# Pairing the projections of three rounds in one hybrid decoder layer: product 1 of two pairs in seven quarter products instead of eight

## The chip, the cores and the metric

One kernel launch on one core of a Trainium2 chip. The metric is the device time of one execution in microseconds; the times are medians of several executions. Engines are named as in the profile: PE is TensorE, DVE VectorE, ACT ScalarE, POOL GpSimd, SP the queue that issues most DMAs.

## The reference

One decoder layer on a prompt of 1024 tokens and 8 sample tokens (1032 columns in the kernel, activations transposed: model dimension on partitions), model width 1024, all in f32:

```python
x = layer_norm(ALPHA * x + 0.5 * swiglu(x, ffn1_wi, ffn1_wo), ...)
z = x @ w_in + b_in          # [q | k | v | o-gate | i | f | B | C | h | gate_a | gate_b], 1024 columns each but i, f (4)
y_a = (HeadLN(mLSTM(q, k / 16, v, i, f)) * sigmoid(o)) @ w_a
y_b = (B * conv3(C * h)) @ w_b                 # causal depthwise convolution over tokens, width 3
x = layer_norm(ALPHA * x + (sigmoid(g_a) * y_a + sigmoid(g_b) * y_b) @ w_mix, ...)
x = layer_norm(ALPHA * x + 0.5 * swiglu(x, ffn2_wi, ffn2_wo), ...)
x = layer_norm(ALPHA * x + sigmoid(x @ w_pg) * (p @ w_pp), ...)
```

The change lies in `z = x @ w_in + b_in`.

## The kernel before, in words

**Numbers.** A matmul of f32 operands is done on a high and a low part of each: `w = wh + wl`, `x = xh + xl`, and the three matmuls `wh*xh`, `wh*xl`, `wl*xh` into one accumulator (`product`, lines 575 to 577). A weight tile is split by a cast on ACT (high part) and a subtraction on DVE (low part), the "put" of that tile.

**Pairs.** A projection is done 256 output columns at a time. Such a *pair* is two blocks of 128 outputs, and `pair` (line 581) computes it by a 2x2 split in seven products instead of eight: `wcomb` makes seven weight combinations, the activations `XP` hold seven combinations of token columns, and each of the products 0 to 6 runs for two column blocks s = 0, 1 (256 and 260 columns). A product of one block is 4 row groups of 128 by 3 matmuls, so a pair has 7 x 2 x 12 = 168 matmuls.

**Pairs of pairs.** In the two feed-forward stages, for seven of the blocks each, `pair2` (line 627) does two pairs together (`wcomb2` makes their weights). Product 1 of both uses the same activations, so these two 12-matmul products in two column blocks (48 matmuls) are one 2x2 problem, which is split once more: seven *quarter* products of 6 matmuls, 42 in all, with four tiles of activation combinations `XQ`, which `quarters` builds beforehand on POOL, DVE and ACT. `pair2` accumulates a pair's parts in PSUM tiles `mm`, `aux` and `pn`, copies them to `sreg` or to the target by ACT, and adds later parts on DVE (line 637).

**The ring.** Weight tiles live in a ring of nine slots (`w0` to `w5`, `e0`, `e1`, `cd`), handed out in program order (`slot`). A slot can be filled again when its last reader is done. `XQ` takes three of them (`QS`: `w4`, `w5`, `e0`), so the feed-forward stages run `pair2` on a ring of six.

**The rounds.** The projections q, k, v, B, C and h have four pairs each. Pair 0 of q and k is done first, then `conv(0)` (C, h, B of pair 0; C * h goes into `pre_`, the convolution `conv_y` on DVE makes `y` of it, B multiplies `y`) and `val(0)`. Then three rounds, h = 1, 2, 3, of six `pair` calls each:

```python
    for h in range(1, 4):
        conv(h)
        if h < 3:
            decays(4 * h - 4)
        lin(qscr, Q0, h, AF.Identity, sm=0)
        if h < 3:
            decays(4 * h - 2)
        lin(kscr, K0, h, AF.Identity, 1.0 / 16.0, 1)
        if h == 3:
            dec_pre()
            beside.extend([[] for _ in range(8)] + [[dec_dot]])
        val(h)
```

After them come twelve pairs for the output gate and the merge gates.

**What else uses the ring.** `ahead_all` puts 26 small jobs beside the steps of the rounds (list `beside`, one entry is taken after each product step): each loads a weight block of a later stage into a ring slot (line 192), splits it there (lines 184 and 185) and stores it in DRAM `wscr` (line 197). `decays` takes one slot, loads two broadcast rows (`gscr`), works on them on DVE (line 1359) and ACT, and stores them (`escr`). Since slots are handed out in program order, all jobs of one pair's steps stand in the ring between the weights of that pair and those of the next.

**What sets the order.** A scheduler that simulates the program orders each engine's instructions at build time; on the chip each engine then runs its list in order and waits where an operand is not ready.

Of the kernel before, what the change touches and what calls it, by code (L numbers as in the profile page):

```python
# [11 lines left out]
AF = mybir.ActivationFunctionType  # L12
# [51 lines left out]
def layer_kernel(ctx: ExitStack, tc: tile.TileContext, I, O):  # L64
# [30 lines left out]
    def tmp(n=BM):  # L95
        return tmpp.tile([128, BM], F32, name="tmp", tag="tmp")[:, :n]
# [48 lines left out]
    def use_ring(slots):  # L145
        set_ring([i for i in from_ring() if i in slots])
# [245 lines left out]
    def wcomb(raws):  # L392

        lo_, up = raws
        g = lo_.shape[1]
        a11, a21, a12, a22 = lo_[:, :, 0:128], lo_[:, :, 128:256], up[:, :, 0:128], up[:, :, 128:256]

        def put(src):
            s = slot()
            hi, lo = (s[:, i * 512:i * 512 + g * 128].rearrange("p (k n) -> p k n", n=128) for i in range(2))  # L400
            S.copy(hi, src)  # L401
            V.tensor_tensor(lo, src, F_(hi), op=OP.subtract)  # L402
            return hi, lo

        def fresh():
            return rawp.tile([128, 512], F32, name="raw", tag="raw")[:, :g * 128].rearrange("p (k n) -> p k n", n=128)

        s1, s2, s3 = fresh(), fresh(), fresh()
        out = [put(a11)]
        V.tensor_tensor(s1, a21, a22, op=OP.add)  # L410
        G.tensor_tensor(s3, a11, a21, op=OP.subtract)
        out.append(put(a12))
        V.tensor_tensor(s2, s1, a11, op=OP.subtract)
        out.append(put(s2))
        out.append(put(a22))
        out.append(put(s1))
        s4 = fresh()
        G.tensor_tensor(s4, a12, s2, op=OP.subtract)  # L418
        out.append(put(s3))
        out.append(put(s4))  # L420
        return out
# [66 lines left out]
    def bcol(c0, m):  # L488
        return col(c0 // 128 + m) if c0 < 4096 else col(32 + (c0 - CB0) // 128 + m)
# [516 lines left out]
    XP = x7()  # L1006
# [14 lines left out]
    def sg_pair():  # L1021
        if count["step"] == 0:
            return fixed
        i = 2 * (count["sg"] % 2)
        count["sg"] += 1
        return [gen(psgs[i + q]) for q in range(2)]

    def in_pair(c0):
        i = count["w"]
        count["w"] += 1  # L1030
        return wcomb(wraw(w_in, c0, [praws[1 + (2 * i + q) % 3] for q in range(2)] if count["step"] == 0 else
                          praws[i % 2 * 2:i % 2 * 2 + 2]))


    nT = sb.tile([128, 2, 32], F32, name="nT")
# [180 lines left out]
    def conv_y(j, pre, y):  # L1216
        S.activation(y, pre, AF.Identity, scale=cw(2, j), bias=cbias(j))
        yv, pv = v2(y), v2(pre)
        for sh in (1, 2):
            for d, src in ((yv[:, :, sh:512], pv[:, :, 0:512 - sh]), (yv[:, 1, 0:sh], pv[:, 0, 512 - sh:512])):  # L1220
                V.scalar_tensor_tensor(d, src, cw(2 - sh, j), d, op0=OP.mult, op1=OP.add)
        for r in (1, 0):
            V.scalar_tensor_tensor(smp(y), p24(cbuf[:, j, r:16:2]), cw(r, j), smp(y), op0=OP.mult, op1=OP.add)
        pl = stp.tile([128, 16], F32, name="st", tag="st")[:, 0:10]
        V.tensor_copy(pl[:, 0:2], pre[:, NT - 6:NT - 4])
        V.tensor_copy(p24(pl[:, 2:10]), smp(pre))
        pt = aux()
# [57 lines left out]
        xsums(XP[0], rp, 0, kp)  # L1285
    late_sums(XP[1], rp, ((12, 13, 14, 15), (16, 17, 18, 19)))

    def conv(jj, w=None):
        pre_ = sg_pair()

        def out_c(i, c, fn):
            fn(bs(pre_[i], c, BLK4))

        pair(w or in_pair(CC0 + jj * 256), XP, (0, 1), out_c, w is not None)
        for i in range(2):
            S.activation(pre_[i], pre_[i], AF.Identity, bias=bcol(CC0, 2 * jj + i))

        def out_h(i, c, fn):
            d, t = bs(pre_[i], c, BLK4), tmp(BN[c % 2])
            fn(t)  # L1300
            V.scalar_tensor_tensor(d, t, bcol(CH0, 2 * jj + i), d, op0=OP.add, op1=OP.mult)

        pair(in_pair(CH0 + jj * 256), XP, (0, 1), out_h)
        y = sg_pair()
        for i in range(2):
            conv_y(2 * jj + i, pre_[i], y[i])

        def out_b(i, c, fn):
            d, t = bs(y[i], c, BLK4), tmp(BN[c % 2])
            fn(t)  # L1310
            V.scalar_tensor_tensor(d, t, bcol(CB0, 2 * jj + i), d, op0=OP.add, op1=OP.mult)

        pair(in_pair(CB0 + jj * 256), XP, (0, 1), out_b)
        for i in range(2):
            DQ.dma_start(yscr[2 * jj + i], y[i])

    def lin(dst, c0, n, fn_, scale=1.0, sm=None):

# [11 lines left out]
        return d  # L1330

    def val(h):
        d = lin(None, V0, h, AF.Identity)
        for c in range(8):
            pt = aux(256)
            for i in range(2):
                T.transpose(pt[:, i * 128:(i + 1) * 128], d[i][:, ccol(c):ccol(c) + 128], ident)
            hi, lo = (tmpp.tile([128, BM], R, name="tmp", tag="tmp")[:, :256] for _ in range(2))
            hilo((hi, lo), pt)
            DQ.dma_start(vhscr[h, c], F_(hi))  # L1340
            DQ.dma_start(vlscr[h, c], F_(lo))
# [141 lines left out]

    beside.extend([partial(next, steps, None)] for _ in range(22))
    w_pg, w_pp = I["w_pg"][0], I["w_pp"][0]
    conv(0, w0)
    val(0)
    parts_ = [(w, k, n) for n in range(2) for w, kk in ((w_pg, 8), (w_pp, 2)) for k in range(kk)]
    parts_ += [(I["ffn2_wo"][0], k, n) for n in range(2) for k in (1, 20, 21)]
    ahead_all([w[k * 128:(k + 1) * 128, n * 512:(n + 1) * 512] for w, k, n in parts_], 14 * 14)  # L1490
    for h in range(1, 4):
        conv(h)
        if h < 3:
            decays(4 * h - 4)
        lin(qscr, Q0, h, AF.Identity, sm=0)
        if h < 3:
            decays(4 * h - 2)
        lin(kscr, K0, h, AF.Identity, 1.0 / 16.0, 1)
        if h == 3:
            dec_pre()  # L1500
            beside.extend([[] for _ in range(8)] + [[dec_dot]])
        val(h)

    if count["sg"] % 2:
        psgs = psgs[2:] + psgs[:2]
# [595 lines left out]
```

## Time and profile before

| | |
|---|---|
| median of 3 runs | 2658.96 us (2652.04, 2658.96, 2659.68) |
| profiled execution | 2652.47 us, of which the traced span is 2650.7 us, TensorE clock 0.999 |
| PE busy | 2617.7 us of the span (99%), 21684 matmuls |
| DVE, ACT, POOL busy | 1937.2 (73%), 1286.1 (49%), 686.0 (26%) us |
| three rounds of projections | about 846 to 1200 us after the span's start |
| feed-forward stage with `pair2` | about 140 to 415 us, and again about 1975 to 2250 us |

Busy time is the time in which an engine has an instruction in flight; where PE is busy all the time, the time of a stage is the number of its matmuls times their distance.

### The profile page before, as it was taken

Reading aid. Unit: us, or ns where it says so; the run is one execution under the profiler, and the core shown is the slowest. Engines: PE = TensorE matmul, PEld = TensorE weight load, DVE = VectorE, ACT = ScalarE, POOL = GpSimd, SP = SyncE. Lnnn points to the kernel's source line nnn. Section 1 sums busy time; section 2 is a strip of 40 time slices with the busy share of each in tenths; the row PEclk is TensorE's granted clock in tenths of the full one; section 3 lists DMA queues with packets and bytes.
Section 4 is the critical chain, followed back from the end, with each engine's and each line's share of the span. In section 5 each row is a group of like instructions: output and inputs, shape, how many; then the busy total and the mean of one; then the engine's idle time right before and its main releaser. Section 6 shows DMA issues by size and latency. Waiting matters only on the chain.

```text
span 2650.7 us, 56267 instructions
## 1 busy us (share of the span) xinstructions
PE 2617.7 (99%) x21684; PEld 2579.6 (97%) x21684; DVE 1937.2 (73%) x4239; ACT 1286.1 (49%) x2862; POOL 686.0 (26%) x694
## 2 busy tenths in 40 slices
PE   9999999999999999999999999999999999999998
PEld 9999999999999999999999999999999999999998
DVE  6867667987887758655555678658877667888787
ACT  5444446433554555546566555425544444533241
POOL 2432221112421111111110345323343223111354
PEclk9999999999999999999999999999999999999999
DMA  6333335532234556436667676821433233644421
GB/s 210 96 101 98 99 117 195 181 121 70 73 125 136 189 168 203 152 92 191 199 191 239 225 235 222 255 91 33 145 107 105 92 105 119 221 134 136 174 74 57
DMA packets 319990, 382.96 MB, mean 144 GB/s; under 512 B 29432, under 2 KB 247752, under 8 KB 319720
## 3 DMA queue, kind: packets, MB, share of 16 engines
q1 hardware_dynamic: 297400, 358.10, 41.9%
q10 hardware_dynamic: 22320, 21.26, 2.8%
q8 instruction: 170, 2.79, 0.4%
q14 instruction: 100, 0.82, 0.1%
HBM read 260.26 MB, written 119.05 MB: 143 GB/s over the span
## 4 chain that ended last, share of the span: by engine, by line
PE 85%; DVE 8%; DMA 3%; issue 2%; ACT 2%; POOL 1%; SPq 0%; DVEq 0%; ACTq 0%; POOLq 0%
PE mm L575 15%; PE mm L577 14%; PE mm L576 14%; PE aux L575 6%; PE aux L576 6%; PE aux L577 6%; PE mm L216 5%; PE mm L217 5%; PE mm L218 5%; PE pn L216 1%; PE pn L218 1%; PE pn L217 1%; DVE a L260 1%; DVE a L185 1%; DVE w L402 1%
## 5 line engine op out<-in xcount | busy, mean ns | idle before, releaser
L575 PE MATMUL mm<-a,w 128*128 128x260 f32 (+1 forms) x2348 | 664.2, 283 | 3.3 <-DVE a L878 2.3
L576 PE MATMUL mm<-a,w 128*128 128x260 f32 (+1 forms) x2348 | 660.8, 282 | 0.6 <-DVE a L260 0.5
L577 PE MATMUL mm<-a,w 128*128 128x260 f32 (+1 forms) x2348 | 659.5, 281 | 0.0
L575 PEld LDWEIGHTS mm<-a,w 128*128 128x128 f32 x2348 | 441.7, 188 | 12.2 <-issue 8.0
L576 PEld LDWEIGHTS mm<-a,w 128*128 128x128 f32 x2348 | 442.0, 188 | 1.1 <-DVE a L260 1.0
L577 PEld LDWEIGHTS mm<-a,w 128*128 128x128 f32 x2348 | 441.7, 188 | 0.8 <-issue 0.8
L418 POOL TENSOR_TENSOR raw<-a,raw 128x512 f32<-128x512 f32 (+2 forms) x70 | 86.5, 1236 | 857.8 <-issue 410.7
L575 PE MATMUL aux<-a,w 128*128 128x260 f32 (+1 forms) x814 | 230.7, 283 | 1.0 <-ACT a L259 0.8
L216 PE MATMUL mm<-a,w 128*128 128x260 f32 (+4 forms) x802 | 228.0, 286 | 2.7 <-ACT w L1594 1.9
L576 PE MATMUL aux<-a,w 128*128 128x260 f32 (+1 forms) x814 | 229.2, 282 | 0.0
L577 PE MATMUL aux<-a,w 128*128 128x260 f32 (+1 forms) x814 | 229.1, 281 | 0.0
L217 PE MATMUL mm<-a,w 128*128 128x260 f32 (+4 forms) x802 | 227.7, 285 | 0.6 <-POOL a L1637 0.6
L218 PE MATMUL mm<-a,w 128*128 128x256 f32 (+2 forms) x751 | 213.3, 285 | 0.2 <-DVE w L156 0.2
L575 PE MATMUL mm<-a,e 128*128 128x256 f32 (+1 forms) x681 | 192.8, 283 | 2.8 <-DVE a L878 1.7
L576 PE MATMUL mm<-a,e 128*128 128x256 f32 (+1 forms) x681 | 191.8, 282 | 0.0
L577 PE MATMUL mm<-a,e 128*128 128x256 f32 (+1 forms) x681 | 191.6, 281 | 0.0
L402 DVE TENSOR_TENSOR w<-raw,w 128x512 fp32r<-128x512 f32 (+2 forms) x190 | 129.7, 685 | 55.6 <-ACT w L401 55.3
L401 ACT CAST w<-raw 128x512 fp32r<-128x512 f32 (+2 forms) x190 | 108.8, 574 | 116.7 <-PE mm L577 43.3
L575 PEld LDWEIGHTS aux<-a,w 128*128 128x128 f32 x814 | 153.2, 188 | 3.7 <-issue 2.1
L216 PEld LDWEIGHTS mm<-a,w 128*128 128x128 f32 x802 | 150.8, 188 | 4.8 <-ACT w L1594 3.2
L577 PEld LDWEIGHTS aux<-a,w 128*128 128x128 f32 x814 | 153.3, 188 | 0.0
L576 PEld LDWEIGHTS aux<-a,w 128*128 128x128 f32 x814 | 153.3, 188 | 0.0
(607 smaller groups left out, 8070.8 us busy)
## 6 DMA issues: line engine op xcount, KB each, us to landing
a<-in_ffn_wi_dram SPq DMA_DIRECT2D x80, 512.0 KB
a<-in_w_in_dram SPq DMA_DIRECT2D x68, 512.0 KB
a<-hsum SPq DMA_DIRECT2D x119, 258.0 KB
hsum<-a SPq DMA_DIRECT2D x68, 258.0 KB
a<-in_ffn_wo_dram SPq DMA_DIRECT2D x40, 384.0 KB
wscr<-w SPq DMA_DIRECT2D x23, 512.0 KB
a<-in_state_C_dram ACTq DMA_DIRECT2D x32, 256.0 KB
out_dram<-a ACTq DMA_DIRECT2D x32, 256.0 KB
```

Source lines behind the costliest of these rows:

```text
L185: V.tensor_tensor(lo, F_(lo), F_(hi), op=OP.subtract)
L216: T.matmul(ps, wh, xh, start=(i == 0), stop=False)
L217: T.matmul(ps, wh, xl, start=False, stop=False)
L218: last = T.matmul(ps, wl, xh, start=False, stop=(i == n - 1))
L260: order_["lo"] = V.tensor_tensor(dst[1], src, F_(dst[0]), op=OP.subtract).ins
L401: S.copy(hi, src)
L402: V.tensor_tensor(lo, src, F_(hi), op=OP.subtract)
L418: G.tensor_tensor(s4, a12, s2, op=OP.subtract)
L575: T.matmul(ps, wh, xh, start=start and kp == 0, stop=False, skip_group_check=True)
L576: T.matmul(ps, wh, xl, start=False, stop=False, skip_group_check=True)
L577: T.matmul(ps, wl, xh, start=False, stop=stop and kp == len(xs) - 1, skip_group_check=True)
```

## The change

In the three rounds the six `pair` calls become three `pair2` calls: q with k (`keys`), C with h (inside `conv`), B with v (`conv_val`). `conv(0)` and `val(0)` stay as they were. `XQ` is built beside the B pair of `conv(0)` and `val(0)`, from where on the ring has six slots. Biases move into the copies out of PSUM, k's scale stays an ACT instruction per block, and `times` multiplies in place. After the rounds the ring gets its three slots back, and the part of `XP` that `quarters` overwrote is loaded again (from `x2scr`) and split, as `redo` does in the feed-forward stages.

```diff
+    def times(d, c0, n):
+        def end(i, c, t):
+            e = bs(d[i], c, BLK4)
+            V.scalar_tensor_tensor(e, t, bcol(c0, 2 * n + i), e, op0=OP.add, op1=OP.mult)
+        return end
...
-    def conv(jj, w=None):
+    def conv(jj, w=None, then=None):
         pre_ = sg_pair()
+        if w is None:
+            pair2(wcomb2(in_raw(CC0 + jj * 256), in_raw(CH0 + jj * 256)), XP, XQ, (whole(pre_), own),
+                  (done, times(pre_, CH0, jj)), (lambda i: bcol(CC0, 2 * jj + i), None))
+        else:
...
+    def conv_val(jj, y):
+        d = sg_pair()
+        pair2(wcomb2(in_raw(CB0 + jj * 256), in_raw(V0 + jj * 256)), XP, XQ, (own, whole(d)),
+              (times(y, CB0, jj), done), (None, lambda i: bcol(V0, 2 * jj + i)))
+        for i in range(2):
+            DQ.dma_start(yscr[2 * jj + i], y[i])
+        val_end(jj, d)
+
+    def keys(n):
+        q, k = sg_pair(), sg_pair()
...
+        pair2(wcomb2(in_raw(Q0 + n * 256), in_raw(K0 + n * 256)), XP, XQ, (whole(q), whole(k)), (done, scaled),
+              (lambda i: bcol(Q0, 2 * n + i), None))
+        lin_store(qscr, q, n, 0)
+        lin_store(kscr, k, n, 1)
...
+    late = quarters(XP)
+    XQ = []
+    def then():
+        use_ring([i for i in ring["slots"] if i not in QS])
+        XQ.extend(next(late))
+        beside.extend([partial(next, late)] if i in (3, 8, 19, 24) else [] for i in range(28))
-    conv(0, w0)
+    conv(0, w0, then)
     val(0)
...
     for h in range(1, 4):
-        conv(h)
+        keys(h)
         if h < 3:
             decays(4 * h - 4)
-        lin(qscr, Q0, h, AF.Identity, sm=0)
+        y = conv(h)
         if h < 3:
             decays(4 * h - 2)
-        lin(kscr, K0, h, AF.Identity, 1.0 / 16.0, 1)
-        if h == 3:
+        else:
             dec_pre()
             beside.extend([[] for _ in range(8)] + [[dec_dot]])
-        val(h)
+        conv_val(h, y)
+    set_ring(QS + from_ring())
+    for kp in range(2):
+        t = tmp()
+        DQ.dma_start(t, bs(x2scr[4 + kp], 1, BLK4))
+        hilo(xparts(XP[1], 1, kp), t)
```

Counted over the built programs, PE has 54 matmuls fewer (216 of 256 columns less, 162 of 260 columns more), DVE 117 instructions more, ACT 1 more, POOL 30 more and SP 2 DMAs more.

In the order of the instructions three places matter. First PE at product 1. Before, the product of one pair and one column block (`w_11523` is the weight combination, `a_8682` and its like the activations):

```order
L575 MATMUL aux<-a_8682,w_11523 128x256
L576 MATMUL aux<-a_8682,w_11523 128x256
L577 MATMUL aux<-a_8682,w_11523 128x256
L575 MATMUL aux<-a_8682,w_11523 128x256
L576 MATMUL aux<-a_8682,w_11523 128x256
L577 MATMUL aux<-a_8682,w_11523 128x256
```

and after, one of the seven quarters, here in round 1 of q and k, complete in six matmuls (`w_10713` is a tile of `XQ` in the former slot `w4`):

```order
L575 MATMUL pn<-w_10713,w_11373 128x260
L576 MATMUL pn<-w_10713,w_11373 128x260
L577 MATMUL pn<-w_10713,w_11373 128x260
L575 MATMUL pn<-w_10713,w_11373 128x260
L576 MATMUL pn<-w_10713,w_11373 128x260
L577 MATMUL pn<-w_10713,w_11373 128x260
```

The twelve matmuls of the first kind become six of the second, seven times for two pairs and both column blocks.

Second, PE where the C and h products of round 1 end and the first B product begins. Before (`w_11541` is the last weight of h, `w_11803` the first of B):

```order
L577 MATMUL mm<-a_9407,w_11541 128x260
L575 MATMUL mm<-a_8680,w_11803 128x256
L576 MATMUL mm<-a_8680,w_11803 128x256
L577 MATMUL mm<-a_8680,w_11803 128x256
L575 MATMUL mm<-a_8680,w_11803 128x256
```

and after (`w_11940` last of h, `e_12413` first of B with v):

```order
L577 MATMUL mm<-a_9407,w_11940 128x260
L575 MATMUL mm<-a_8680,e_12413 128x256
L576 MATMUL mm<-a_8680,e_12413 128x256
L575 MATMUL mm<-a_9164,e_12413 128x260
L576 MATMUL mm<-a_9164,e_12413 128x260
L577 MATMUL mm<-a_8680,e_12413 128x256
```

The two matmuls with the high weight part of both column blocks now stand ahead of the first one with the low part.

Third, DVE at the same hand-over. Before, its work on the decays of round 1 (line 1359, `w_12046`), between the convolution (line 1221) and a put of a weight of the q pair (line 402):

```order
L1359 SCALAR_TENSOR_TENSOR w_12046<-w_12046,ga,maskb 128x128
L1221 SCALAR_TENSOR_TENSOR a_11762<-a_11272,pc,a_11762 128x2x511
L1359 SCALAR_TENSOR_TENSOR w_12046<-w_12046,ga,maskb 128x128 x3
L1221 SCALAR_TENSOR_TENSOR a_11763<-a_11273,pc,a_11763 128x1
L1359 SCALAR_TENSOR_TENSOR w_12046<-w_12046,ga,maskb 128x128 x4
L1221 SCALAR_TENSOR_TENSOR a_11762<-a_11272,pc,a_11762 128x1
L1230 COPY tmp<-aux 10x128
L402 TENSOR_TENSOR w_12075<-a_12065,w_12075 128x512
```

and after, the second decays of round 1 (now line 1406, in slot `cd`), ahead of the low part of `e_12413`, with the adds (line 637) and the multiplications (line 1301) of the h pair between:

```order
L1406 SCALAR_TENSOR_TENSOR cd<-cd,ga,maskb 128x128 x2
L637 TENSOR_TENSOR sreg<-sreg,mm 128x260 x2
L1301 SCALAR_TENSOR_TENSOR a_11860<-sreg,pc,a_11860 128x256
L1406 SCALAR_TENSOR_TENSOR cd<-cd,ga,maskb 128x128 x2
L1301 SCALAR_TENSOR_TENSOR a_11860<-sreg,pc,a_11860 128x256
L1406 SCALAR_TENSOR_TENSOR cd<-cd,ga,maskb 128x128 x4
L330 TENSOR_TENSOR e_12413<-a_12399,e_12413 128x512
```

The eight decay instructions, and with them their DMA, now stand ahead of the put of the next product's weight.

More of the change, by code (lines that the diff above doesn't have):

```diff
@@ L1026, in sg_pair, with in_raw, in_pair @@
         return [gen(psgs[i + q]) for q in range(2)]
-    def in_pair(c0):
+    def in_raw(c0):
         i = count["w"]
         count["w"] += 1
-        return wcomb(wraw(w_in, c0, [praws[1 + (2 * i + q) % 3] for q in range(2)] if count["step"] == 0 else
+        return (wraw(w_in, c0, [praws[1 + (2 * i + q) % 3] for q in range(2)] if count["step"] == 0 else
                           praws[i % 2 * 2:i % 2 * 2 + 2]))
+    def in_pair(c0):
+        return wcomb(in_raw(c0))
     nT = sb.tile([128, 2, 32], F32, name="nT")
@@ L1286, in layer_kernel, with whole, own, done @@
     late_sums(XP[1], rp, ((12, 13, 14, 15), (16, 17, 18, 19)))
-    def conv(jj, w=None):
-        pre_ = sg_pair()
[L1291 to L1303, printed above, removed]
+    def whole(d):
+        return lambda i, c: bs(d[i], c, BLK4)
+    def own(i, c):
+        return None
+    def times(d, c0, n):
[3 more added lines that the diff above has]
+        return end
+    def done(i, c, t):
+        pass
+    def conv(jj, w=None, then=None):
+        pre_ = sg_pair()
+        if w is None:
+            pair2(wcomb2(in_raw(CC0 + jj * 256), in_raw(CH0 + jj * 256)), XP, XQ, (whole(pre_), own),
+                  (done, times(pre_, CH0, jj)), (lambda i: bcol(CC0, 2 * jj + i), None))
+        else:
+            def out_c(i, c, fn):
+                fn(bs(pre_[i], c, BLK4))
+            pair(w, XP, (0, 1), out_c, True)
+            for i in range(2):
+                S.activation(pre_[i], pre_[i], AF.Identity, bias=bcol(CC0, 2 * jj + i))
+            def out_h(i, c, fn):
+                d, t = bs(pre_[i], c, BLK4), tmp(BN[c % 2])
+                fn(t)
+                V.scalar_tensor_tensor(d, t, bcol(CH0, 2 * jj + i), d, op0=OP.add, op1=OP.mult)
+            pair(in_pair(CH0 + jj * 256), XP, (0, 1), out_h)
         y = sg_pair()
@@ L1306, in conv @@
             conv_y(2 * jj + i, pre_[i], y[i])
+        if then is None:
+            return y
+        then()
         def out_b(i, c, fn):
@@ L1315, in conv, with scaled @@
             DQ.dma_start(yscr[2 * jj + i], y[i])
+    def conv_val(jj, y):
+        d = sg_pair()
+        pair2(wcomb2(in_raw(CB0 + jj * 256), in_raw(V0 + jj * 256)), XP, XQ, (own, whole(d)),
+              (times(y, CB0, jj), done), (None, lambda i: bcol(V0, 2 * jj + i)))
+        for i in range(2):
+            DQ.dma_start(yscr[2 * jj + i], y[i])
+        val_end(jj, d)
+    def keys(n):
+        q, k = sg_pair(), sg_pair()
+        def scaled(i, c, t):
+            S.activation(t, t, AF.Identity, scale=1.0 / 16.0, bias=bcol(K0, 2 * n + i))
+        pair2(wcomb2(in_raw(Q0 + n * 256), in_raw(K0 + n * 256)), XP, XQ, (whole(q), whole(k)), (done, scaled),
+              (lambda i: bcol(Q0, 2 * n + i), None))
+        lin_store(qscr, q, n, 0)
+        lin_store(kscr, k, n, 1)
     def lin(dst, c0, n, fn_, scale=1.0, sm=None):
@@ L1332, in val, with val_end @@
     def val(h):
-        d = lin(None, V0, h, AF.Identity)
+        val_end(h, lin(None, V0, h, AF.Identity))
+    def val_end(h, d):
         for c in range(8):
```

## The prediction

> **What bounds the kernel now.** The page's first part and the chain that ended last come first: they say which engine sets the time.
>
> ```profile
> span 2650.7 us, 56267 instructions
> PE 2617.7 (99%) x21684; PEld 2579.6 (97%) x21684; DVE 1937.2 (73%) x4239; ACT 1286.1 (49%) x2862; POOL 686.0 (26%) x694
> PE 85%; DVE 8%; DMA 3%; issue 2%; ACT 2%; POOL 1%; SPq 0%; DVEq 0%; ACTq 0%; POOLq 0%
> ```
>
> PE is the bound, and a share is an average, so the second view is that of stretches: one inside the first feed-forward stage, which already runs `pair2` on a ring of six, the three rounds of projections, and the hand-over from C and h to B in round 1.
>
> ```profile
> core 0: us, PE busy (x) PEld busy (x) DVE busy (x) ACT busy (x) POOL busy (x), PEclk, DMA share, GB/s
> 250.00:450.00 200.00, 200.00 (x1686) 200.00 (x1686) 139.68 (x293) 96.88 (x228) 49.37 (x44) 1.00 0.36 116
> 860.00:1200.00 340.00, 340.00 (x2871) 339.45 (x2869) 229.66 (x489) 178.09 (x383) 47.57 (x35) 1.00 0.51 159
> 880.00:900.00 20.00, 20.00 (x171) 19.97 (x170) 20.00 (x50) 8.88 (x20) 2.96 (x2) 1.00 0.45 154
> ```
>
> In the rounds PE never pauses: 2871 matmuls in 340.00 us are one per 118.4 ns, as in the feed-forward stretch (200.00 / 1686 = 118.6 ns), at the full granted clock. So a matmul that goes is worth its distance, if nothing new makes PE wait. DVE is busy 68% of the rounds, but in the last row all of its 20 us: there the convolution, the decays and the puts come together. PE lives through that on the ring's reserve, which the change cuts.
>
> **What PE saves.** 54 matmuls go. At 118.4 ns each they are 6.4 us; since the quarters are all 260 wide, by columns it is 216 x 256 - 162 x 260 = 13176 columns at 118.4 / 258 = 0.459 ns, 6.05 us. I take 6.1. It is also the most that the change can bring: 0.23%.
>
> **What the other engines get.** DVE: 36 adds more, 18 puts of 512 fewer but 63 of 256 more, 18 more sums of 256, some 18 instructions for `quarters`.
>
> ```profile
> L402 DVE TENSOR_TENSOR w<-a,w 128x512 fp32r<-128x512 f32 x23 | 15.7, 684 | 5.5 <-ACT w L401 5.5
> L597 DVE TENSOR_TENSOR a<-sreg,aux 128x256 f32<-128x256 f32 x11 | 4.5, 411 | 0.2 <-PE aux L577 0.2
> L330 DVE TENSOR_TENSOR w<-a,w 128x256 fp32r<-128x256 f32 x9 | 3.6, 422 | 12.5 <-ACT w L329 12.5
> L401 ACT CAST w<-a 128x512 fp32r<-128x512 f32 x24 | 15.0, 624 | 17.0 <-PE mm L577 8.5 <-PE aux L577 6.0 <-DMA wscr<-w 2.0
> ```
>
> 36 x 0.41 - 18 x 0.68 + (63 + 18) x 0.42 + 18 x 0.42 = 44 us, some 36 of them in the rounds, which brings DVE there from 68% to (229.66 + 36) / 334 = 80%. ACT gets 63 casts of 256 for 18 of 512 and loses six passes over a whole tile, some 8 us in all on an engine that is busy 178 of 340 us. By themselves these cost nothing as long as the average counts; where DVE is full already they do (below). `quarters` is built in 28 steps beside B of `conv(0)` and `val(0)`; the same builder ran in the feed-forward stages and left PE at 100%, so I cost it at nothing (if its last piece were late, PE would wait one put, about 1.3 us). The stores of q to DRAM must be out before the C product overwrites their tiles. Their last element is made in the quarters; 145 matmuls, 17 us, lie between that and the first overwrite. Five such stores are issued in 2.90 us (first row below), so eight in 4.6, and with the 3.2 us that a store takes to land (further below) that is 8 us: hidden, no cost taken; uncovered it would be those 8 us once per round. SP's two extra DMAs are the reload at the end, which the two feed-forward stages show (second row, a wait of PE):
>
> ```profile
> 912.84 2.90 SPq L1243 DMA_DIRECT2D qscr<-a  x5
> PE aux L575 <- ACT a L259: 0.8, 1, 0.8
> ```
>
> That wait is in the second stage, and the first shows none. I take 0.4 us, with 0 and 0.8 as ends.
>
> **What the ring of six costs.** In the feed-forward stage one turn of slot `e1` was this (of the first row the first start, of the last read of the old content; of the last row the first start, of the first read of the new):
>
> ```profile
> L577 PE MATMUL mm<-a,e x10: 279/282/287, 277.3 to 286.9; 128*128 128x260 f32 x6, 128*128 128x256 f32 x4
> L329 ACT CAST e<-raw x1: 621/621/621, 278.0 to 278.0; 128x512 fp32r<-128x512 f32 x1
> L330 DVE TENSOR_TENSOR e<-raw,e x1: 692/692/692, 278.6 to 278.6; 128x512 fp32r<-128x512 f32 x1
> L575 PEld LDWEIGHTS mm<-a,e x8: 187/188/192, 282.6 to 286.5; 128*128 128x128 f32 x8
> ```
>
> Released at 277.6, cast at 278.0, low part ready at 279.3, first read at 282.6: 3.3 us of reserve, the smallest that I found there. In the rounds the ring also carries other things: by program order, four `ahead` jobs and a decays stand between the weights of q, k and those of C, h, three jobs and a decays before B, v, three jobs before the next q, k. With a ring of six that leaves almost nothing: the first weight of C waits for the very last product of k. What such a job holds a slot for:
>
> ```profile
> 906.97 0.35 SPq L192 DMA_DIRECT2D w<-in_w_pg_dram  x1
> 910.59 0.62 ACT L184 CAST w<-w 128x512 fp32r<-128x512 f32 x1 [3.03 <-DMA w<-in_w_pg_dram]
> 892.56 0.33 SPq L197 DMA_DIRECT2D wscr<-w  x1
> 895.75 0.62 ACT L401 CAST w<-raw 128x512 fp32r<-128x512 f32 x1 [0.74 <-DMA wscr<-w]
> 898.61 0.83 SPq L1356 DMA_DIRECT2D w<-gscr  x2
> 902.79 1.13 DVE L1359 SCALAR_TENSOR_TENSOR w<-w,ga,maskb 128x128 f32<-128x128 f32 x4
> ```
>
> Load 3.6 us, cast and subtraction 1.3, store 3.2, together 8.1 us, and the next put 1.3. Between the release ahead of a job and the use of the slot behind it, the new order has 101 matmuls (12.0 us) or more, so the jobs just fit. The decays do not quite. At C, h to B, v the slot of `e_12413` comes free 24 matmuls before the end, but its low part stands behind eight decay instructions. Their load (line 1403) is queued on SP behind the store of `w_12129`, whose slot comes free 88 matmuls (10.4 us) before the end: 10.4 - 3.6 - 1.3 = 5.5 us before the end the load can go, 4.2 us later the first decay starts (898.61 to 902.79), 1.3 us before the end. Eight of them at 0.28 (1.13 / 4), four adds and multiplications at about 0.35 and the subtraction at 0.68 take 4.3 us: the low part is there 3.0 us after the end, or 1.8 if the load takes 3.6 us and two of the adds are done while it is awaited. PE has four matmuls, 0.5 us, to do without it. So it waits 1.3 to 2.5 us; I take the middle, 1.9, in rounds 1 and 2, together 3.8 us. At q, k to C, h the decays' load can go 2.8 us before the end, and the low part of C's first weight behind them is there -2.8 + 4.2 + 2.2 + 1.4 = 5.0 us after it; there the order has 52 matmuls (6.2 us) ahead that can do without it. On time, but only just.
>
> Then the full DVE. In round 1 a put that began with the cast at 895.75 got its low part only here:
>
> ```profile
> 900.32 0.68 DVE L402 TENSOR_TENSOR w<-raw,w 128x512 fp32r<-128x512 f32 x1
> ```
>
> 5.25 us instead of 1.3 (until 901.00). The excess, 3.9 us, against 3.3 us of reserve is 0.6 us of waiting; I take 0.5 once per round, 1.5 us. The ends are 0 and 3.0 per place: the new order has slots with only 19 matmuls (2.25 us) between release and next use, at two places of a round.
>
> These rows speak against all added POOL work:
>
> ```profile
> 871.42 1.41 POOL L418 TENSOR_TENSOR raw<-a,raw 128x512 f32<-128x512 f32 x1 [16.75 <-issue]
> 871.21 1.90 DVE L1301 SCALAR_TENSOR_TENSOR a<-tmp,pc,a 128x256 f32<-128x256 f32 x2
> 874.46 1.29 POOL L411 TENSOR_TENSOR raw<-a 128x512 f32<-128x512 f32 x1 [1.63 <-DVE e L402]
> 874.63 1.40 DVE L1301 SCALAR_TENSOR_TENSOR a<-tmp,pc,a 128x260 f32<-128x260 f32 x1
> 876.57 0.48 DVE L1301 SCALAR_TENSOR_TENSOR a<-tmp,pc,a 128x260 f32<-128x260 f32 x1
> 896.48 0.88 DVE L1311 SCALAR_TENSOR_TENSOR a<-tmp,pc,a 128x260 f32<-128x260 f32 x2
> ```
>
> One multiplication takes 0.48 us undisturbed, two 0.88 (the last two rows). While POOL was at work one took 1.40 and two took 1.90: 0.9 and 1.0 us lost to one POOL instruction. The Trainium skill ("SBUF — State Buffer", section on the two separate sides) says more: a DVE instruction with two SBUF inputs and a POOL instruction that reads SBUF hold a shared port in turn, the whole instruction long. The rows agree, though not with the whole 1.29 and 1.41 us; by that rule alone the 18 added POOL instructions of the rounds would cost DVE up to 18 x 1.35 = 24 us, by the rows 18 x 0.95 = 17 us, and the sum below holds neither, since DVE has 20% to spare on the mean.
>
> **Sum.** -6.1 + 3.8 + 1.5 + 0.4 = -0.4 us against the profiled execution (2652.47 us, 1.8 us around its span): 2652.1 us. That execution lies 6.5 us under the median of the runs shown, so on the median's scale it is 2658.6 us. No change: 0.3% is 8.0 us, and three runs of one kernel spread over 7.6 us, so less than that can hardly be told here.
>
> **Rivals.** *All stays covered.* DVE's mean of 80% and the scheduler's reordering (high parts first) suffice, and PE runs through as in the feed-forward stage. Then -6.1, 2652.9 us. For it: 100% PE there on six slots with DVE at 70%. Against it: there the ring carried weights alone.
>
> *The ring starves PE: slower.* In each round the 19-matmul places meet a DVE with 5.25 us per put: 5.25 - 2.25 = 3.0 us, at two places in three rounds 18 us, so 2658.96 - 6.1 + 18 = 2670.9 us. It decides from 3.3 us per put on (2.25 + 6.1 / 6), which the full 20 us of the last window row make credible; against it, that row is 20 of a round's 119 us (1008 matmuls).
>
> *POOL takes DVE's time.* Six POOL instructions lie in each B, v pair, beside the burst, where two pairs had four; at 0.9 to 1.0 us and over three rounds, all 18 are 17 us of DVE time, the added 6 are 6. If half to all of the added time, and a little of the rest, reaches PE, some 7 us come on top of my sum: 2665.6 us.
>
> That the matmuls don't go is excluded by the count.
>
> **Chances.** My sum (-4 to +4 around the median, 2655 to 2663 us) 0.42; all covered 0.24; starved 0.22; POOL 0.08; the rest, unforeseen waits at the hand-over, 0.04. Less than 2651.0 us (faster by over 0.3%) needs the covered case and a low draw of the runs: 0.24 x 0.35 + 0.42 x 0.12 = 0.13. More than 2666.9 us: 0.8 of the starved, half of POOL and of the rest, a little of mine: 0.25. Between: 0.62. The range runs from 2648 (covered, low draw) to 2671 us (starved).
>
> **What the profile after will show.** PE with 54 matmuls fewer. In the windows of the rounds either 100% again (covered) or waits of product lines for the put's DVE line: at the first B, v product of rounds 1 and 2, 1.3 to 2.5 us each, behind line 1406 (my sum), none in round 3; or at the quarters and weights 2 and 3 of the second pair in all rounds (starved). DVE in the rounds near 80%. A wait for `gscr` or `wscr` at q, k to C, h, or waits for PSUM tiles because DVE's adds come late, would make the sum wrong; so would the quarters' build if PE waits at the first of them.

## The result: 0.7% slower, and the profile after

| | before | after |
|---|---|---|
| median | 2654.53 us (2652.04 to 2659.68) | 2675.22 us (2670.27 to 2675.95) |
| ratio | | 1.0072, 95% interval 1.0061 to 1.0083 |
| profiled execution, span | 2652.47, 2650.7 us | 2670.27, 2668.5 us |

The forecast was 2658.6 us, no change, with a range up to 2671 us; the measured median lies 4 us above the range. With more runs the median of before came down from 2658.96 to 2654.53 us, so the change itself is +20.7 us where -0.4 was forecast. The two profiled executions, on which the readings below rest, lie 17.8 us apart: that of after is the fastest of its six, so about 3 us of the 20.7 stand in no trace.

First the head of the page after, then three stretches of it (columns as in the prediction): B of `conv(0)` with `val(0)`, where the quarters are built; the rounds; the end of the rounds with the reload.

```profile
span 2668.5 us, 56293 instructions
PE 2620.9 (98%) x21630; PEld 2580.2 (97%) x21630; DVE 1993.2 (75%) x4356; ACT 1277.5 (48%) x2863; POOL 717.7 (27%) x724
800.00:840.00 40.00, 34.66 (x273) 34.41 (x273) 36.09 (x73) 16.35 (x38) 18.47 (x16) 0.91 0.21 67
860.00:1200.00 340.00, 332.50 (x2761) 329.91 (x2760) 263.00 (x571) 163.97 (x366) 62.33 (x50) 0.99 0.52 161
1200.00:1240.00 40.00, 36.94 (x296) 36.28 (x296) 25.86 (x51) 20.69 (x44) 6.44 (x5) 0.96 0.54 165
```

The 54 matmuls are gone, but PE is busy 3.2 us longer, and in 340 us of the rounds it gets through 2761 matmuls where it did 2871. In the first row the granted clock is 0.91, in the last 0.96: PE pauses, and it also runs slower. From the 6500th matmul to the 10300th (10246th, where 54 are fewer) before took 451.8 us and after 471.1; the rest of the program is the same within 1.5 us. The waits of PE in 700 to 1260 us that before did not have there (total us, times, longest; one of 0.2 us is left out):

```profile
PE aux L575 <- ACT sreg L604: 5.3, 1, 5.3
PE mm L577 <- DVE e L330: 4.9, 2, 2.5
PE aux L575 <- ACT a L259: 2.4, 1, 2.4
PE mm L575 <- DVE sreg L637: 1.3, 2, 0.9
PE mm L577 <- DVE w L330: 0.9, 2, 0.7
PE aux L1384 <- DVE tmp L260: 0.6, 2, 0.4
```

Three places make 12.6 us. The first is the build of the quarters, the second the B, v hand-over of rounds 1 and 2, the third the reload.

**The build.** From here on rows of single instructions (start, duration, engine, line, operation). DVE and POOL while PE waits, the release, and last a low part with POOL idle:

```profile
816.20 1.71 POOL L352 TENSOR_TENSOR raw<-a 128x512 f32<-128x512 f32 x1
816.71 1.48 DVE L260 TENSOR_TENSOR e<-tmp,e 128x260 fp32r<-128x260 f32 x1
818.27 0.85 POOL L303 TENSOR_TENSOR tmp<-a 128x260 f32<-128x260 f32 x1 [0.36 <-DVE e L260]
818.45 0.95 DVE L260 TENSOR_TENSOR w<-tmp,w 128x260 fp32r<-128x260 f32 x1
819.55 1.05 POOL L304 TENSOR_TENSOR tmp<-tmp 128x260 f32<-128x260 f32 x1 [0.43 <-DVE w L260]
819.93 0.95 DVE L260 TENSOR_TENSOR w<-tmp,w 128x260 fp32r<-128x260 f32 x1
820.92 0.42 DVE L612 SCALAR_TENSOR_TENSOR tmp<-sreg,mm 128x256 f32<-128x256 f32 x1
821.45 0.37 ACT L604 COPY sreg<-aux 128x256 f32<-128x256 f32 x1 [0.41 <-DVE tmp L612]
821.88 0.58 PE L575 MATMUL aux<-a,w 128*128 128x260 f32 x1 [5.34 <-ACT sreg L604]
822.00 0.42 DVE L260 TENSOR_TENSOR e<-tmp,e 128x260 fp32r<-128x260 f32 x1
```

PE needs a PSUM tile `aux`; ACT can empty it only into an `sreg` that DVE has read (line 612); and that read stands on DVE behind the convolution and the quarters. A low part of 260 elements (line 260) takes 0.42 us when POOL is idle; here it takes 0.95 to 1.48.

**The hand-over** in round 1: the decays (1406), then the low part of `e_12413` (330), then PE. It is the order shown under "The change".

```profile
920.83 0.61 DVE L1406 SCALAR_TENSOR_TENSOR cd<-cd,ga,maskb 128x128 f32<-128x128 f32 x2 [0.90 <-DMA cd<-gscr]
921.36 0.76 DVE L637 TENSOR_TENSOR sreg<-sreg,mm 128x260 f32<-128x260 f32 x2
922.17 0.39 PE L575 MATMUL mm<-a,e 128*128 128x260 f32 x1 [0.35 <-DVE sreg L637]
923.35 1.13 DVE L1406 SCALAR_TENSOR_TENSOR cd<-cd,ga,maskb 128x128 f32<-128x128 f32 x4
924.40 0.68 DVE L330 TENSOR_TENSOR e<-a,e 128x512 fp32r<-128x512 f32 x1
925.14 0.38 PE L577 MATMUL mm<-a,e 128*128 128x256 f32 x1 [2.46 <-DVE e L330]
```

The short waits for line 637 belong to the same place: the adds that free the PSUM tile stand behind the first decay instructions, which wait for their load; PE waits 0.35 us for them here and 0.95 us in round 2. So it is with the waits for `w L330`, 0.71 and 0.22 us: they lie at q, k to C, h, behind the other decays.

**The reload** (line 1560) is issued on SP behind the stores of v, and its cast on ACT comes after a table load (ACT_TABLE_LOAD) and a sigmoid of the first gate pair:

```profile
1228.84 0.28 SPq L1396 DMA_DIRECT2D vscr<-tmp  x1
1231.11 0.81 SPq L1560 DMA_DIRECT2D tmp<-x2scr  x2
1232.98 1.28 ACT L1369 ACT_TABLE_LOAD   x1
1234.28 0.51 ACT L1369 ACTIVATE a<-a,pc 128x256 f32<-128x256 f32 x1
1234.69 0.70 ACT L259 CAST a<-tmp 128x260 fp32r<-128x260 f32 x2
```

In the trace the two loads land at 1233.8 and 1234.1 us, so the table load and the sigmoid held the first cast by at most 0.9 us; the rest is the late issue and the load itself.

**The clock.** Stretches of 2 us around the first wait; the column after POOL's is the granted clock:

```profile
816.00:818.00 2.00, 0.54 (x5) 0.33 (x3) 2.00 (x2) 0.00 (x0) 1.91 (x2) 1.00 0.23 78
818.00:820.00 2.00, 0.00 (x0) 0.00 (x0) 2.00 (x5) 0.41 (x1) 1.30 (x2) 0.91 0.00 0
820.00:822.00 2.00, 0.12 (x1) 0.12 (x1) 1.97 (x6) 0.95 (x3) 0.60 (x1) 0.50 0.00 0
822.00:824.00 2.00, 2.00 (x10) 2.00 (x11) 2.00 (x7) 0.54 (x2) 0.00 (x0) 0.50 0.02 4
824.00:826.00 2.00, 2.00 (x11) 2.00 (x11) 2.00 (x6) 0.90 (x2) 1.09 (x2) 0.50 0.00 0
826.00:828.00 2.00, 2.00 (x17) 2.00 (x17) 2.00 (x5) 0.37 (x1) 1.57 (x2) 0.88 0.00 0
828.00:830.00 2.00, 2.00 (x19) 2.00 (x18) 1.60 (x4) 1.34 (x4) 1.04 (x2) 1.00 0.66 264
```

After the pause PE counts as fully busy but does 10 or 11 matmuls in 2 us instead of 19, at a clock of 0.50. The same follows each of the other three waits. In all, 67 matmuls stand some 0.217 us apart instead of 0.118, which loses 6.4 us. Together: 12.6 + 6.4 + 3.3 (short waits behind the start of the rounds) - 6.1 = 16.2 of the 19.3 us. Of the other 3 us, 2.0 lie at the same waits, twelve in all (from start to start of the matmuls a wait costs some 0.16 us more than the idle time that the profile counts); the rest is spread over matmuls a little further apart.

### The profile page after: what moved, and what is told of

The parts are those of the page before. It is cut to its first block, busy times and chain, and to the rows that moved or that the text cites. A ratio compares the mean times of both kernels' runs of the same rounds, so it can differ in the third digit from the quotient of the medians.

```text
span 2668.5 us, 56293 instructions
## 1 busy us (share of the span) xinstructions
PE 2620.9 (98%) x21630; PEld 2580.2 (97%) x21630; DVE 1993.2 (75%) x4356; ACT 1277.5 (48%) x2863; POOL 717.7 (27%) x724
## 4 chain that ended last, share of the span: by engine, by line
PE 50%; DVE 7%; DMA 3%; ACT 1%; issue 1%; POOL 0%; SPq 0%; DVEq 0%; ACTq 0%; POOLq 0%
PE mm L575 8%; PE mm L577 8%; PE mm L576 8%; PE mm L216 4%; PE mm L217 3%; PE mm L218 3%; PE aux L575 3%; PE aux L576 3%; PE aux L577 3%; PE pn L216 1%; PE pn L218 1%; DVE a L260 1%; PE pn L217 1%; PE pn L575 1%; DMA raw<-in_w_a_dram 1%
## 5 line engine op out<-in xcount | busy, mean ns | idle before, releaser
L575 PE MATMUL mm<-a,w 128*128 128x260 f32 (+1 forms) x2308 | 651.1, 283 | 3.6 <-DVE a L878 2.2
L576 PE MATMUL mm<-a,w 128*128 128x260 f32 (+1 forms) x2308 | 648.9, 282 | 0.3
L577 PE MATMUL mm<-a,w 128*128 128x260 f32 (+1 forms) x2308 | 645.5, 282 | 0.9 <-DVE w L330 0.9
L575 PEld LDWEIGHTS mm<-a,w 128*128 128x128 f32 x2308 | 434.2, 188 | 8.8 <-issue 3.4
L576 PEld LDWEIGHTS mm<-a,w 128*128 128x128 f32 x2308 | 434.5, 188 | 0.7 <-DVE a L260 0.7
L577 PEld LDWEIGHTS mm<-a,w 128*128 128x128 f32 x2308 | 433.0, 188 | 2.0 <-DVE w L330 1.3
L575 PE MATMUL aux<-a,w 128*128 128x260 f32 (+1 forms) x856 | 243.5, 285 | 8.2 <-ACT sreg L604 5.3
L576 PE MATMUL aux<-a,w 128*128 128x260 f32 (+1 forms) x856 | 242.2, 283 | 0.0
L577 PE MATMUL aux<-a,w 128*128 128x260 f32 (+1 forms) x856 | 242.1, 283 | 0.0
L575 PE MATMUL mm<-a,e 128*128 128x260 f32 (+1 forms) x721 | 206.1, 286 | 4.1 <-DVE a L878 1.8
L217 PE MATMUL mm<-a,w 128*128 128x260 f32 (+4 forms) x734 | 209.7, 286 | 0.2
L216 PE MATMUL mm<-a,w 128*128 128x260 f32 (+4 forms) x734 | 208.7, 285 | 0.6 <-DVE a L913 0.6
L577 PE MATMUL mm<-a,e 128*128 128x260 f32 (+1 forms) x721 | 204.4, 284 | 4.9 <-DVE e L330 4.9
L218 PE MATMUL mm<-a,w 128*128 128x260 f32 (+3 forms) x739 | 208.5, 285 | 0.2 <-DVE w L156 0.2
L576 PE MATMUL mm<-a,e 128*128 128x260 f32 (+1 forms) x721 | 204.6, 284 | 0.0
L575 PEld LDWEIGHTS aux<-a,w 128*128 128x128 f32 x856 | 162.2, 190 | 10.0 <-ACT sreg L604 5.5
L577 PEld LDWEIGHTS aux<-a,w 128*128 128x128 f32 x856 | 162.6, 190 | 0.0
L576 PEld LDWEIGHTS aux<-a,w 128*128 128x128 f32 x856 | 162.5, 190 | 0.0
L329 ACT CAST w<-raw 128x512 fp32r<-128x512 f32 (+1 forms) x182 | 98.2, 548 | 113.8 <-PE mm L577 49.3
L575 PEld LDWEIGHTS mm<-a,e 128*128 128x128 f32 x721 | 137.6, 191 | 7.0 <-issue 2.3
L360 POOL TENSOR_TENSOR raw<-a,raw 128x512 f32<-128x512 f32 x46 | 63.1, 1372 | 298.7 <-issue 134.7
```

Source lines behind the costliest of these rows:

```text
L216: T.matmul(ps, wh, xh, start=(i == 0), stop=False)
L217: T.matmul(ps, wh, xl, start=False, stop=False)
L218: last = T.matmul(ps, wl, xh, start=False, stop=(i == n - 1))
L329: S.copy(dst[0], src)
L360: G.tensor_tensor(s2, blocks(r)[2], s2, op=OP.subtract)
L575: T.matmul(ps, wh, xh, start=start and kp == 0, stop=False, skip_group_check=True)
```

## The experiments

Theory A: the time went to these three places, at each a wait and then a slow clock. Its rivals: B, DVE or the short ring is too full everywhere, so that a mended wait comes up elsewhere; C, the slow clock has nothing to do with the waits. The bracketed numbers are ratios to the kernel before, run beside each kernel, with their intervals; "less" is against the 2675.22 us of the result, taken in another session (before had 2654.53 us there and 2655.15 to 2655.51 us beside the experiments).

**Each place alone, and all three.**

```
- beside.extend([partial(next, late)] if i in (3, 8, 19, 24) else [] for i in range(28))
+ beside.extend([partial(next, late)] if i in (14, 18, 22, 26) else [] for i in range(28))
```

> The four pieces of the quarters' build are taken after steps 14, 18, 22 and 26 instead of 3, 8, 19 and 24, so after the convolution of conv(0) has left DVE; all else as in the changed kernel (2675.2 us). Theory A (three places, each a wait and then a slow clock): the wait of 5.3 us at the second product of B in conv(0) goes, and with it the 20 slow matmuls behind it (1.9 us): 7.2 us less, 2668.0 us. Rival B (DVE as a whole is too full, the ring starves PE): the same DVE work only moves, PE waits as long elsewhere: 2673 to 2676 us. Rival C (the slow clock does not come from the wait): only the wait goes, 2669.9 us, and matmuls at half clock stay somewhere near 820 us.

Measured 2668.25 us (1.0050, 1.0036 to 1.0063), 7.0 less. The 5.3 us wait is gone; a new one of 1.5 us stands at the transposes of `val(0)`.

```
...
-        keys(h)
-        if h < 3:
-            decays(4 * h - 4)
+        if h < 3:
+            for at, c0 in ((0, 4 * h - 4), (24, 4 * h - 2)):
+                beside[at + 3].append(partial(decays_load, c0))
+                beside[at + 10].append(partial(decays_work, c0))
+        keys(h)
...
```

> Each decays is parted into a load and its work, taken beside steps 3 and 10 of keys and of conv in rounds 1 and 2, as the ahead jobs are, instead of standing between two pairs. All else as in the changed kernel (2675.2 us). Theory A: the two waits of 2.5 us at the first B, v product go, and the slow clock behind them (30 matmuls, 3.0 us), with a half of the 1.1 us that stand beside the second: 8 us less, 2667 us. Rival B: the work of the decays is the same and now lies in the middle of a pair; waits of the same size come up there, 2673 to 2677 us. Rival C: 4.9 us less, 2670.3 us.

Measured 2664.87 us (1.0029, 1.0017 to 1.0041), 10.4 less. Both waits for `e L330` and the slow clock behind them are gone, and with them the waits for line 637 and all but 0.2 us of those for `w L330`: which fits a gain above the 8 us expected. A new one shows, at the hand-over from q, k to C, h; on ACT a cast of line 329 just ahead of it waited for the store of an `ahead` job:

```profile
PE mm L575 <- ACT w L329: 1.8, 3, 1.5
```

```
+            beside.extend([] for _ in range(17 - len(beside)))
+            beside.extend([[partial(again, kp)] for kp in range(2)])    # again: the reload's three lines
         conv_val(h, y)
...                                                                      # and no reload behind the rounds
```

> The reload of the overwritten part of XP is taken beside steps 17 and 18 of the last B, v pair, behind the last quarter product, instead of behind all work of that pair. All else as in the changed kernel (2675.2 us). Theory A: the wait of 2.4 us at the first pair after the rounds goes, with the 17 slow matmuls behind it (1.6 us): 4.0 us less, 2671.2 us. Rival B: DVE and ACT are no fuller there than before, so B expects no more than 1 us: 2674 us. Rival C: 2.4 us less, 2672.8 us.

Measured 2669.34 us (1.0050, 1.0038 to 1.0062), 5.9 less; no wait for line 259 is left.

> The three edits of the other runs together. Theory A: the sum, 7.2 + 8 + 4.0 = 19.2 us less than the changed kernel, 2656.0 us, as the kernel before (2654.5 us) within 0.3%; no matmuls at half clock between 800 and 1260 us. Rival B: at most a third of it, 2669 to 2676 us, with the waits at other lines of the rounds. Rival C: 12.7 us less, 2662.5 us.

Measured 2657.94 us (1.0005, 0.9996 to 1.0013), 17.3 less, and no matmul at half clock between 800 and 1260 us. A stands; B (2669 or more) falls, and so does C (2662.5). The three single gains add up to 23.3 us against 17.3 together; with some 3 us of uncertainty in each, that is no contradiction, but the single sizes are not exact.

**What makes the build's wait long.** The same place as in the change, but POOL's share of the build on DVE:

```
-                G.tensor_tensor(x, F_(b[:, h]), F_(b[:, l]), op=OP.add)
+                (G_ or G).tensor_tensor(x, F_(b[:, h]), F_(b[:, l]), op=OP.add)    # and lines 304, 314, 315
...
-    late = quarters(XP)
+    late = quarters(XP, V)
```

> The build of the quarters in conv(0) and val(0) at its old place (after steps 3, 8, 19, 24), but its 12 POOL instructions (lines 303, 304, 314 and 315) on DVE; all else as in the changed kernel (2675.2 us; 2668.5 us span in its profile). In the changed kernel DVE's six instructions that ran beside POOL between 811.3 and 820.9 us took 7.1 us instead of 2.8. Theory P (POOL takes DVE's time): the 8 POOL instructions of the first two pieces come to DVE with 0.34 us each, 2.7 us, and 4.3 us of slowing go: the wait of 5.3 us shrinks to 3.7 us or less, with the slow clock behind it 2673 us at the most. Rival W (DVE simply has too much work there): the wait grows by 2.7 to 8.0 us, 2678 us.

Measured 2669.86 us (1.0055, 1.0041 to 1.0069).

```profile
PE aux L575 <- ACT sreg L604: 3.5, 1, 3.5
```

DVE got more work, and the wait became 1.8 us shorter. (The total fell by 5.4 us, more than the wait and its slow clock explain, but its interval is 3.7 us wide to either side, and the two profiled executions differ by 0.7 us only.) POOL did take DVE's time there. The wait did not vanish: DVE is crowded there by the convolution and the build, and two POOL sums of weights still held two DVE instructions (1.74 instead of 0.68 us, 1.50 instead of 0.42).

**Whether the pause makes the slow clock.** Twenty matmuls more fill the wait at the two hand-overs:

```
+            if idles:
+                for _ in range(idles.pop()):
+                    T.matmul(ps, wh, xh, start=True, stop=True, skip_group_check=True)
             T.matmul(ps, wh, xh, start=start and kp == 0, stop=False, skip_group_check=True)
...
+        if h < 3:
+            idles.append(20)
         conv_val(h, y)
```

> Ahead of the first B, v product of rounds 1 and 2, 20 matmuls more write into the same PSUM tile with a start flag, so their result is overwritten by the first real matmul. They take 20 x 0.118 = 2.37 us, just the wait of 2.46 us that stands there; all else as in the changed kernel (2675.2 us). Theory A (the slow clock comes from the pause): PE stays busy, the granted clock stays at 1.00 there, and the 30 slow matmuls go: 3.0 us less, 2672.2 us, though PE has 40 matmuls more. Rival C (the slow clock has another cause): slow matmuls stay, 2675 us. Rival D (the wait is PE's own and only shifted): 4.7 us more, 2680 us.

Measured 2667.97 us (1.0048, 1.0036 to 1.0061): with 40 matmuls more it is 7.2 us faster. The first hand-over again, in 2 us stretches, with the row of the added matmuls (their minimum, median and maximum duration, first and last start):

```profile
922.00:924.00 2.00, 2.00 (x20) 2.00 (x19) 2.00 (x8) 0.91 (x2) 0.00 (x0) 1.00 0.56 229
924.00:926.00 2.00, 1.50 (x13) 1.29 (x12) 2.00 (x7) 1.81 (x4) 0.00 (x0) 1.00 0.19 72
926.00:928.00 2.00, 2.00 (x19) 2.00 (x19) 2.00 (x5) 1.14 (x2) 0.00 (x0) 1.00 0.85 152
L579 PE MATMUL mm<-a,e x20: 278/279/281, 921.9 to 924.1; 128*128 128x256 f32 x20
```

The clock stays at 1.00 where it was 0.50, and the low part comes no sooner (DVE is done with it at 925.3 us, 925.1 without the added matmuls). So at these places the slow clock is the pause's doing; C and D fall. The gain is larger than the 3.0 us expected, because in this run the reload's wait was 0.5 us instead of 2.4, with no slow clock after it (together 3.5 us); why it came earlier there is not shown.

**Whether the ring of six starves PE.** The kernel before, only with the shorter ring:

```
+    use_ring([i for i in ring["slots"] if i not in QS])
     for h in range(1, 4):
         conv(h)
...
+    set_ring(QS + from_ring())
```

> The kernel before (2655 us), with its six pair calls per round unchanged, but on the ring of six in the three rounds (w4, w5 and e0 lie idle). Theory A (the ring of six by itself does not starve PE; only the decays at a hand-over can be late): 0 to 3 us more, 2655 to 2658 us. Rival S (the short ring starves PE, as my second rival had it): 10 us more or above, 2665 us or more.

Measured 2657.97 us (1.0010, 1.0001 to 1.0018): 2.7 us more than before. The short ring alone is no cause of 20 us. It is not free either: the stretch of the rounds takes 456.0 us instead of 451.8.

**Where the 6.1 us have gone.** With the three places mended the kernel is as fast as before, not faster. First the pieces of the build still later:

```
- beside.extend([partial(next, late)] if i in (14, 18, 22, 26) else [] for i in range(28))
+ beside.extend([partial(next, late)] if i in (20, 27) else [] for i in range(28))
...
+    beside[4].append(partial(next, late))        # steps of round 1
+    beside[9].append(partial(next, late))
```

> As the kernel with all three edits (2657.9 us), but the pieces of the quarters still later: after steps 20 and 27 of B and val, and after steps 4 and 9 of keys in round 1, just ahead of the first quarter product. Theory A: of the waits left between 700 and 1260 us, 1.5 us for line 1369 at the transposes of val(0) and some 0.5 us more go: 2656 us. Rival B (DVE is too full, the ring starves PE): the pieces now meet the ahead jobs of round 1 and PE waits there: 2660 us or more.

Measured 2652.74 us (0.9993, 0.9984 to 1.0001), better than expected. The rounds' stretch takes 452.0 us, still what it took before (451.8).

Two tries to take more out missed. In one the `ahead` jobs start at fixed steps of each pair2:

```
- at = i * (steps - 8) // len(srcs)
+ at = i // 3 * 24 + (0, 7, 14)[i % 3]
```

> As the kernel with the later pieces (2652.7 us), but the 26 ahead jobs start at steps 0, 7 and 14 of each pair2 instead of every 7.2 steps, so none has its slot across a hand-over. Theory A (what is left are single waits at the hand-overs): the wait of 1.3 us for line 329 at keys to C, h in round 1 goes and perhaps one of the 0.9 us: 2651 us. Rival B (DVE or the ring as a whole): the waits move, 2652 to 2655 us.

2662.90 us (1.0027, 1.0017 to 1.0037): a wait of 2.0 us for a cast of line 329 with a slow clock behind it now stands at the B, v hand-over of round 3. In the other POOL's share of the build goes to DVE as well (the edit shown above), at the later place:

> As the one with aligned jobs, and the 12 POOL instructions of the quarters' build on DVE. At the later place DVE has room, so theory P expects little there: 0 to 1 us less than the aligned one, 2650 to 2651 us. Rival W (more DVE work costs PE time wherever it is): 2 us more, 2653 us or above.

> As the kernel with the later pieces (2652.7 us), with the 12 POOL instructions of the quarters' build on DVE. Theory P: the aligned pair of kernels showed 2.8 us less for this edit; here 1 to 2 us less, 2651 us. Rival W: 1 us more, 2654 us.

2660.12 us (1.0019, 1.0010 to 1.0027) with the aligned jobs, and 2654.31 us (0.9999, 0.9991 to 1.0008) without them: once 2.8 us less, once 1.6 more, neither beyond the scatter. Away from the convolution POOL's part does not matter measurably.

Then the jobs out of the rounds, all 26 beside the gate pairs behind them (the rest, here and below, as in the 2652.74 us kernel):

```
-    ahead_all([...], 14 * 14)        # ahead of the rounds
...
+    ahead_all([...], 168)            # ahead of the twelve gate pairs
```

> As the kernel with the later pieces (2652.7 us), but the 26 ahead jobs run beside the twelve gate pairs after the rounds, on the ring of nine, and none beside the rounds. Theory A with the ring (what is left of waits in the rounds comes from jobs that hold slots of the short ring at hand-overs): the waits for lines 329 and 330 in the rounds go, 1.7 us or a little more; the gate pairs, where the DMA engines are busy 70%, take it with at most 1 us: 2651 us. Rival E (nothing in the rounds hangs on the jobs): the rounds stay and the gate pairs lose: 2655 us or more.

2657.12 us (1.0006, 0.9997 to 1.0014). The total, 6 us above what was expected, says nothing gained; the stretches say where it went: the rounds, and the start of the gate pairs.

```profile
860.00:1200.00 340.00, 340.00 (x2872) 339.64 (x2872) 253.21 (x568) 161.41 (x357) 64.49 (x52) 1.00 0.37 108
1240.00:1300.00 60.00, 56.27 (x420) 49.29 (x419) 37.94 (x93) 31.74 (x69) 8.41 (x7) 0.94 0.82 252
PE pn L1511 <- DVE a L1498: 3.4, 1, 3.4
```

The rounds run through, 445.6 us for the stretch, 6.2 less than before: the whole of the 54 matmuls. The gate pairs lose it; the largest piece is one wait of 3.4 us with its slow clock. Two more runs place the jobs otherwise. First all 26 start 40 steps later in the gate pairs:

```
- at = i * (steps - 8) // len(srcs)
+ at = 40 + i * (steps - 48) // len(srcs)
```

> As the one with the jobs beside the gate pairs (2657.1 us; its rounds ran through, 6 us faster than those of before, and one pause of 3.4 us with its slow clock stood in the first gate pairs, 2657.0 us span), but the jobs begin 40 steps into the gate pairs. Theory A: the pause at the first gate pairs goes, 4.5 us less, 2652.5 us or, if the 6 us of the rounds come through whole, 2650 us. Rival E (26 jobs beside the gate pairs cost what they cost beside the rounds, by the DMA engines' traffic there): another pause, 2656 us or more.

2652.45 us (0.9983, 0.9973 to 0.9994), rounds 447.0 us; the wait of 3.4 us is 1.2 us now, without a slow clock. Then eight of them back in the rounds:

```
+        for i in range(8):
+            at = i * 24 + 10           # one job in the middle of each of eight pair2, the other 18 from step 40 of the gate pairs
```

> One ahead job in the middle of each of eight pair2 (step 10), and the other 18 beside the gate pairs from step 40 on. Theory A (jobs at a hand-over of the short ring make the waits, not jobs as such): the rounds run as without jobs, 6 us faster than those of before, and the gate pairs have less than in the other kernel: 2650 us. Rival B (any job on the short ring costs PE time): the rounds stay 3 us behind, 2653 us or more.

2648.79 us (0.9974, 0.9963 to 0.9984), rounds 445.3 us: 6.7 us faster than before (2655.51 in the same comparison), 4.2 to 9.8 by the interval, and the 54 matmuls' 6.1 us lie in it. (The kernel before was not run with its jobs placed this way; its stretch of the rounds had no wait to lose.)

```profile
span 2647.5 us, 56327 instructions
PE 2614.1 (99%) x21630; PEld 2575.3 (97%) x21630; DVE 1996.5 (75%) x4356; ACT 1279.2 (48%) x2863; POOL 717.6 (27%) x724
860.00:1200.00 340.00, 340.00 (x2871) 339.67 (x2870) 262.04 (x579) 167.03 (x367) 65.90 (x52) 1.00 0.41 126
```

DVE has as much work here as in the slow kernel (1996.5 against 1993.2 us) and PE never waits in this stretch. So it was not the amount of DVE's work, but what stood in front of what. For the jobs that is not shown: eight in the middle of the pairs cost the rounds nothing (445.3 us against 445.6 with none), 26 spread over them some 6 us (452.0), but number and place were changed together, and three per pair at fixed steps were worse (458.0).

## Why the prediction was wrong, point by point

- *54 matmuls, -6.1.* Right: 6.2 to 6.5 us in the rounds' stretch of the two runs where nothing pauses there.
- *"the same builder ran in the feed-forward stages and left PE at 100%, so I cost it at nothing".* The step that failed most: 5.3 us of wait and 1.9 of slow clock, 7.0 measured by moving it. The likeness was false. Beside the builder of the first feed-forward stage (110 to 140 us of before; the row quoted was of 250 to 450 us) DVE was busy 23.05 of 30 us, and PE had a wait of 0.5 us even there. At the new place, with the convolution, DVE was full before anything was added, as this row of before shows:

```profile
800.00:820.00 20.00, 20.00 (x170) 19.96 (x169) 19.81 (x42) 7.31 (x16) 2.57 (x2) 1.00 0.32 104
```

The price was looked for at the last piece ("one put"), not at the adds that empty PSUM.

- *Decays ahead of the first B, v put.* Place, rounds and mechanism right, round 3 free of it as said. Too small: 2.46 us each, the upper end of the 1.3 to 2.5; I took the middle. With the slow clock the term of 3.8 was 7.8 us by the trace. What the decays also held up was put at nothing: the adds for PSUM at the same place (1.3 us) and the weights at q, k to C, h, "on time, but only just" (0.9 us late). Together that is 10.0 us, and undoing it brought 10.4.
- *Reload, 0.4 with 0 and 0.8 as ends.* 2.4 us and 1.6 of slow clock. The ends were taken from the feed-forward stages, one wait of 0.8 us; here a row of stores on SP, a table load and a sigmoid on ACT stand ahead of it. The instruction was priced, its neighbours in the queues were not.
- *Full DVE, 1.5.* Near in size by luck: there were 2.2 us of waits for lines 637 and 330, but all behind decays, in rounds 1 and 2 only, and gone when the decays were moved (but for 0.2 us). No wait of the forecast kind, a put late at a place with 19 matmuls, once per round, was found. DVE's share came out at 263.00 / 340 = 77% (forecast 80%).
- *A term that the sum did not have:* the slow clock, 6.4 us. In the stretches shown of before the clock was 1.00 throughout, so no row priced a pause beyond its own length. The ends of the other terms, and so the top of the range, lacked it too.
- *Rival "starved", 2670.9.* Nearest in time, wrong in cause: the ring alone costs 2.7 us, and the only waits for weights in the rounds were those behind the decays. *Rival "POOL takes DVE's time".* The mechanism is real, but it cost PE time at the build (4.3 us of DVE's in six instructions), not in the rounds, where I had priced it: the 2648.79 us kernel has as much POOL work in the rounds (65.90 us) and no wait. *"All covered"* was possible, with the jobs and the three places moved: 2648.8 us against its 2652.9.
- *Stores of q before C's product overwrites them: hidden.* Right, no such wait.

## What to carry to other kernels

A piece of work that was free in one stage is priced anew in another: look at what stands ahead of it in each queue there (DVE, ACT and SP each had something), above all at the instructions that empty PSUM. Row loads with work on DVE belong in the middle of a long product, not at the hand-over between two: moved there, with load and work apart, the decays lost their waits (which of the two did it was not separated). Where PE is the bound, a pause of about 2 us mostly brings the slow clock with it, so price it at its length and some 1 to 2.5 us more; a change worth 0.2% shows only when such pauses are gone.

## What the runs showed of the hardware

**A pause costs more than its length.** Between 700 and 1300 us of all these traces PE waited 20 times for 1.9 us or longer; 19 times matmuls some 0.217 us apart followed, for 2.4 to 5.8 us, losing 1.1 to 2.6 us. One wait of 2.34 us went by without it (`e5_pool`, at the reload). Single waits of 1.2 to 1.8 us there did not bring it. The length alone does not decide, though: in the stage at 1530 us the same wait (line 215 for line 1665) was 1.41 us long in `e12_gates` and was followed by the slow clock, and 2.29 us long in `e13_gates40` and was not. In each trace the changes of the granted clock lie whole multiples of 3.41 us apart, and in these stretches it stood at 0.50 for 3.41 or 6.83 us. The Trainium skill ("TensorE: Matmul & The Clock Gate", Part 1: The HAM clock gate) says that the array falls to half clock after an idle window of about 3.4 us and is released after as long a busy one, with windows that run freely. The clock of 0.50 and the steps of 3.41 us agree; the pauses needed here were shorter than the 3.4 us that it warns of, down to 1.41.

**POOL holds DVE up to the end of its instruction.** In the rows of the build POOL ends at 817.91, 819.12 and 820.60 us, and the DVE instruction with two SBUF inputs that began meanwhile ends at 818.19, 819.40 and 820.88: each time 0.28 us later. The prediction had it that the rows agree with the rule of the Trainium skill ("SBUF — State Buffer", SBUF: two separate sides) only in part; these three agree with it whole. So do the prediction's own two, which it read wrongly: POOL ends at 872.83 and 875.75 us, DVE at 873.11 and 876.03, again 0.28 us later.
